# Two heads in one step: row-paired products of GLA and mLSTM inside a float32 block stack

## The chip, the cores and the metric

The kernel runs on one core of one Trainium2 chip. The metric is device time in microseconds (us), the median of several runs of the whole program, which is one launch. TensorE is called PE below, VectorE DVE, ScalarE ACT, GpSimd POOL and SyncE SP, as in the profile. All inputs and the output are float32.

## The reference, cut to what matters

Two blocks follow each other on one sequence of 1024 tokens of width 1024. The first is a recurrent mixer with its projections. The second holds a mixer with three branches (GLA, mLSTM, S5) and a feed-forward part. The change touches the two branches GLA and mLSTM, each with 4 heads whose keys and queries are 64 wide and whose values are 128 wide. In the reference they read

```python
# GLA, per chunk and head
o_inter = jnp.einsum('bhld,bhdv->bhlv', qi * jnp.exp(cum), state)
scores = jnp.einsum('bhid,bhjd,bhijd->bhij', qi, ki, decay)
o = o_inter + jnp.einsum('bhij,bhjv->bhiv', scores, vi)
# mLSTM, per chunk and head
scores = jnp.einsum('bhtd,bhsd->bhts', qi, ki) * jnp.exp(d_intra - m_t[..., None])
num = (w_inter[..., None] * jnp.einsum('bhtd,bhdv->bhtv', qi, mem)
       + jnp.einsum('bhts,bhsv->bhtv', scores, vi))
den = w_inter * jnp.einsum('bhtd,bhd->bht', qi, norm) + jnp.sum(scores, axis=-1)
h = num / jnp.maximum(jnp.abs(den), jnp.exp(-m_t))[..., None]
```

Products over the 64 key channels (scores, and query times state) contract 64 rows; products of the scores with the values contract the 128 tokens of a chunk.

## The kernel before, in words

The kernel works on 8 chunks of 128 tokens. A head pair (`hp` 0 or 1) shares one tile of 128 partitions: partitions 0 to 63 hold the key channels of head `h` = 0 of the pair, partitions 64 to 127 those of `h` = 1. A slice `r` picks one half, so a product over key channels uses one half of the array's rows.

The large projections are products of split float32 operands: each takes three products of 128 rows (`mm3`, L2457), and they form the main stream, whose PSUM tiles are named `mm` (4 buffers). GLA and mLSTM are generators that run beside that stream. The order of PE is written by hand: it executes in the order in which the Python code emits. After every 2500 ns of estimated main products (`tick` and `slot`, L2373 and L2382; usually 12 products of 512 columns) the generator at the head of the list `side` advances by one `yield`, at a rate of 1.08 per slot, so that about every 12th slot advances it twice without main work between. Generators in the list `fast` advance in every slot. The order of the other engines' instructions, and of the DMA queue on SP, comes from the framework's scheduler. Products outside the main stream go to PSUM tiles named `sm` (4 buffers, L2419). One float32 product shows as two records on PE, one for each pass.

GLA (`gla`, L1144) builds the score matrix of a head in 8 levels. `scores(l, h, wk, wq)` (L1181) makes, for one level and one head, two groups of four chunk products, each group in its own `sm` buffer, and copies each group into the tile `P` of that head: with a masked copy on DVE (L1203) for level 7 and levels 2 to 6, with ACT copies for levels 0 and 1 (whose products have 64 and 32 columns). There is a `yield` after each head. `weights` prepares the operand tile `w` of the next level. After the levels, for each head and each half of the chunks (`n4`), a product of `P` with the values `gv` (128 rows) and, for all but the first chunk, a product of the state (`S`, allocated as tile `kd`) with `qe` (allocated as tile `g`; 64 rows) accumulate alternately into one `sm` buffer. `head_norm` (L518) squares and scales that result into a tile `C`, and later transposes it.

mLSTM (`mlstm`, L1312) has eight steps per head pair, four per head, in a software pipeline: step `n` emits the scores of step `n` (`score`, L1454: two 64-row products into one buffer, then one DVE product into `mP`), the transposes of step `n`-2 (`finish`, L1484, from `mhn` into `my`), and the outputs of step `n`-1 (`numden`, L1465: 128-row products of `mP` with `mv`, and 64-row products of the state `mS` with `qw`, allocated as `mraw`, alternately), then yields. After the outputs, ACT takes an absolute value into `mdn`, DVE a maximum, a reciprocal and a product into `mhn`, which `finish` transposes. `rows_of` (L1391) loads the decay rows `mD` and the gate `mo` of a head.

Of the kernel before, what the change touches and what calls it, by code (L numbers as in the profile page):

```python
# [16 lines left out]
P = 128  # L17
# [103 lines left out]
class PhaseA:  # L121
# [395 lines left out]

    def head_norm(self, o, n, scale, dst, sp):  # L518

        ss = sp.tile([P, 4], F32, tag="hss", name=self.name("hss"), bufs=2)  # L520
# [12 lines left out]
        self.act(dst, ps[:, : n * P], AF.Copy)  # L533
# [10 lines left out]
class PhaseB:  # L544
# [599 lines left out]
    def gla(self):  # L1144
# [4 lines left out]
        def t_(name, shape, bufs=1):  # L1149
            return pool.tile([P] + list(shape), F32, tag=name, name=self.name(name), bufs=bufs)  # L1150
# [27 lines left out]
            self.mul(pr(w)[:, :, B : 2 * B], pr(d)[:, :, B : 2 * B], pr(q)[:, :, B : 2 * B])  # L1178
            return w

        def scores(l, h, wk, wq):  # L1181
            r = slice(h * 64, h * 64 + 64)
            B = LEVELS[l] if l < 7 else 0
            for n4 in range(2):
                ps = self.sm_ps()
                pt = pts[h][:, n4 * 4 : n4 * 4 + 4]
                p4 = ps.rearrange("p (n c) -> p n c", n=4)
                for j in range(4):
                    c0 = (n4 * 4 + j) * P
                    if B == 64:  # L1190
                        self.mm(p4[0:64, j, 64:P], wk[r, c0 : c0 + 64], wq[r, c0 + 64 : c0 + P])
                    elif B == 32:
                        for o in (0, 64):
                            self.mm(p4[o : o + 32, j, o + 32 : o + 64], wk[r, c0 + o : c0 + o + 32], wq[r, c0 + o + 32 : c0 + o + 64])
                    else:
                        self.mm(p4[:, j], wk[r, c0 : c0 + P], wq[r, c0 : c0 + P])
                if B == 64:
                    self.act(pt[0:64, :, 64:P], p4[0:64, :, 64:P], AF.Copy)
                elif B == 32:
                    for o in (0, 64):  # L1200
                        self.act(pt[o : o + 32, :, o + 32 : o + 64], p4[o : o + 32, :, o + 32 : o + 64], AF.Copy)
                else:
                    nc.vector.copy_predicated(pt, lm[:, l - 2].unsqueeze(1).broadcast_to([P, 4, P]), p4)  # L1203

        for hp in range(2):
            while ("gk", hp) not in self.zdone or "rows" not in self.zdone:
# [46 lines left out]
            yield  # L1253
            for l in range(7):
                nw = weights(l + 1, cum, q, k) if l < 6 else None
                for h in range(2):
                    scores(l, h, w, w)
                    yield
                    if l == 0:

                        if h == 0:
                            S = t_("kd", [T])
                        ps = self.sm_ps()
                        part = range(4 * h, min(4 * h + 4, NCH - 1))
# [13 lines left out]
                    yield  # L1278
                w = nw
            yield  # L1280
            for h in range(2):
                head = 2 * hp + h
                while ("gr", head) not in self.zdone:
                    yield
                r = slice(h * 64, h * 64 + 64)
                y = t_("w", [T], 2)
                gr, t = t_("d" if h else "kt", [T]), t_("e2", [T])
                nc.sync.dma_start(gr, self.z["gr"][head])
                norms = []
                for n4 in range(2):  # L1290
                    o = self.sm_ps()
                    for j in range(4):
                        n = n4 * 4 + j
                        oj = o[:, j * P : j * P + P]
                        self.mm(oj, pts[h][:, n], v[:, n, h * P : h * P + P], True, n == 0)
                        if n:
                            self.mm(oj, qe[r, n * P : n * P + P], S[r, n * P : n * P + P], False, True)
                    norms.append(self.head_norm(o, 4, 1.0 / P, y[:, n4 * H : n4 * H + H], pool))
                    next(norms[-1])
                    yield  # L1300
                self.act(t, gr, AF.Tanh, scale=0.5)
                self.stt(t, t, 1.0, gr, ALU.add, ALU.mult)
                for f in norms:
                    yield
                    for _ in f:
                        pass
                self.stt(y, y, self.col("gla_norm_w_2", head), t, ALU.mult, ALU.mult)
                nc.sync.dma_start(self.yd["gla"][head], y)
        pool.release()


    def mlstm(self):  # L1312
# [78 lines left out]
        def rows_of(head):  # L1391
# [9 lines left out]
            return d, mo, t_("my", [T], 2)  # L1401

        for hp in range(2):
            mk = yield from conv("mk", hp)
# [24 lines left out]
                    )  # L1429
            while ("mo", 2 * hp + 1) not in self.zdone:  # L1430
                yield
            nxt = rows_of(2 * hp)
            yield
            qw = t_("mraw", [T + 4], 2)[:, :T]
            for h in range(2):
                nc.sync.dma_start(qw[h * 64 : h * 64 + 64], bd[1, 2 * hp + h : 2 * hp + h + 1].broadcast_to([64, T]))
            self.stt(qw, mq, 0.5, qw, ALU.mult, ALU.mult)
            yield
            S = t_("mS", [NCH, 130])
            for n0 in range(0, NCH - 1, 3):  # L1440
                part = range(n0, min(n0 + 3, NCH - 1))
# [9 lines left out]
                yield  # L1451


            def score(h, n2, D):  # L1454
                r = slice(h * 64, h * 64 + 64)
                sc = self.sm_ps()
                pt = t_("mP", [2, P], bufs=2)
                for j in range(2):
                    n = n2 * 2 + j
                    c = slice(n * P, n * P + P)  # L1460
                    self.mm(sc[:, j * P : j * P + P], mk[r, c], mq[r, c])
                self.stt(pt.rearrange("p n c -> p (n c)"), sc[:, :256], 2.0 ** -5, D[:, n2 * 256 : n2 * 256 + 256], ALU.mult, ALU.mult)
                return pt

            def numden(h, n2, pt):  # L1465
                head = 2 * hp + h
                r = slice(h * 64, h * 64 + 64)
                o = self.sm_ps().rearrange("p (n c) -> p n c", n=2)
                for j in range(2):
                    n = n2 * 2 + j  # L1470
                    c = slice(n * P, n * P + P)
                    self.mm(o[:, j, 0:130], pt[:, j], v[h][:, n], True, n == 0)
                    if n:
                        self.mm(o[:, j, 0:130], qw[r, c], S[r, n], False, True)

                dn = t_("mdn", [2], bufs=2)
                self.act(dn, o[:, :, P], AF.Abs)
                self.tt(dn, dn, cols[:, 2, n2 * 2 : n2 * 2 + 2, head], ALU.max)
                nc.vector.reciprocal(out=dn, in_=dn)
                hn = t_("mhn", [2, P], bufs=2)  # L1480
                self.mul(hn, o[:, :, 0:P], dn.unsqueeze(2).broadcast_to([P, 2, P]))
                return hn

            def finish(h, n2, hn, mo, y):  # L1484
                ps = self.sm_ps()
                for j in range(2):
                    self.tr(ps[:, j * P : j * P + P], hn[:, j])
                c = slice(n2 * 256, n2 * 256 + 256)
                self.stt(y[:, c], mo[:, c], 1.0, ps[:, :256], ALU.add, ALU.mult)
                if n2 == 3:  # L1490
                    nc.sync.dma_start(self.yd["ml"][2 * hp + h], y)

            steps = [(h, n2) for h in range(2) for n2 in range(4)]
            have = {}
            for n in range(len(steps) + 2):
                if n < len(steps):
                    h, n2 = steps[n]
                    if n2 == 0:
                        have[h] = nxt
                        if h == 0:  # L1500
                            nxt = rows_of(2 * hp + 1)
                    have["pt", n] = score(h, n2, have[h][0])
                if n >= 2:
                    h, n2 = steps[n - 2]
                    finish(h, n2, have.pop(("hn", n - 2)), *have[h][1:])
                if 1 <= n <= len(steps):
                    have["hn", n - 1] = numden(*steps[n - 1], have.pop(("pt", n - 1)))
                yield
        pool.release()


# [1066 lines left out]
```

## Time and profile before

| what | value |
|---|---|
| median of 3 runs | 2270.28 us (2265.58 to 2273.81) |
| the profiled execution: its time | 2265.43 us |
| the profiled execution: its span, first to last instruction | 2263.6 us |
| mean granted PE clock over the span | 0.986 of full speed |
| PE busy | 2192.0 us, 97% of the span |
| DVE busy | 1514.4 us, 67% |
| ACT busy | 903.3 us, 40% |
| POOL busy | 394.7 us, 17% |

A row of a timeline gives the start from the span's start and the length in us, the engine, the line, the operation, the tile written and the tiles read, the shapes, and the number of records merged into the row; in brackets stands the idle time of the engine just before, and what ended it. The length of a PE row goes to the end of its last record, and records overlap, so the distance from one start to the next tells what a record costs. All PE products go through two helper lines, L2455 (matmul) and L2464 (transpose), so tile names tell them apart: `sm<-w` are GLA's scores of levels 0 to 6, `sm<-gq,gk` those of level 7, `sm<-gv,P` and `sm<-kd,g` GLA's outputs, `sm<-mq,mk` mLSTM's scores, `sm<-mv,mP` and `sm<-mS,mraw` its outputs, `sm<-ident,mhn` its transposes.

### The profile page before, as it was taken

The numbers are of one execution on the slowest core, as the hardware profiler recorded it, in microseconds if no ns is written. First come the engines' busy times: TensorE is split into PE (matmuls) and PEld (weight loads), VectorE is DVE, ScalarE is ACT, GpSimd is POOL, SyncE is SP. The second block draws the span as 40 slices with busy tenths as digits, with TensorE's granted clock in tenths as the row PEclk, the third lists the DMA queues.
The fourth block names the chain that finished last, engine by engine and source line by source line (L and its number), as shares of the span: only waits on it lengthen the run. The fifth ranks groups of instructions, "written<-read, shape, count | busy, mean of one in ns | idle before, by whom it ended". The sixth has DMA issues, their size and how long they took to land.

```text
span 2263.6 us, 29466 instructions
## 1 busy us (share of the span) xinstructions
PE 2192.0 (97%) x10998; PEld 1807.4 (80%) x10998; DVE 1514.4 (67%) x2160; ACT 903.3 (40%) x1522; POOL 394.7 (17%) x388
## 2 busy tenths in 40 slices
PE   8999999999999999999999999999799999999896
PEld 7888788887888988878887778887578888887676
DVE  6675686777486535558555346858977676779697
ACT  5553453344255544234253222446423232334343
POOL 1000000001112200000000000011745343425245
PEclk9999999999999999999999999999899999999998
DMA  4111116321743343255454255654233222267754
GB/s 172 34 44 40 40 51 205 103 61 29 224 144 115 98 145 136 98 170 166 152 172 143 79 183 181 202 180 153 88 123 110 84 84 84 98 228 253 246 177 160
DMA packets 149815, 297.59 MB, mean 131 GB/s; under 512 B 21520, under 2 KB 43936, under 8 KB 149416
## 3 DMA queue, kind: packets, MB, share of 16 engines
q1 hardware_dynamic: 135128, 271.33, 37.2%
q0 software_dynamic: 8128, 20.07, 2.5%
q10 hardware_dynamic: 6416, 4.31, 0.7%
q8 instruction: 87, 1.43, 0.3%
q14 instruction: 56, 0.46, 0.1%
HBM read 232.55 MB, written 61.90 MB: 130 GB/s over the span
## 4 chain that ended last, share of the span: by engine, by line
PE 76%; DVE 10%; DMA 5%; issue 5%; ACT 2%; POOL 2%; SPq 0%; POOLq 0%; ACTq 0%; DVEq 0%
PE mm L2455 56%; PE sm L2455 19%; DVE lo L2423 2%; DVE al L2423 1%; PE sm L2464 1%; DVE sc L2423 1%; DMA c<-ffa 1%; DVE res L2435 1%; DVE acc L2423 1%; POOL res L1843 1%; ACT hi L2449 0%; DVE B L2435 0%; DVE rl L2435 0%; DMA raw<-in_wfo 0%; ACT C L2449 0%
## 5 line engine op out<-in xcount | busy, mean ns | idle before, releaser
L2455 PE MATMUL mm<-rh,hi 128*128 128x512 f32 x1552 | 625.6, 403 | 1.1 <-DVE res L2423 0.7
L2455 PE MATMUL mm<-rl,hi 128*128 128x512 f32 x1552 | 606.2, 391 | 1.8 <-DVE rl L2423 1.8
L2455 PE MATMUL mm<-rh,lo 128*128 128x512 f32 x1552 | 606.7, 391 | 0.0
L2455 PEld LDWEIGHTS mm<-rh,hi 128*128 128x128 f32 x1552 | 292.5, 188 | 72.8 <-issue 9.5
L2455 PEld LDWEIGHTS mm<-rh,lo 128*128 128x128 f32 x1552 | 292.2, 188 | 62.8
L2455 PEld LDWEIGHTS mm<-rl,hi 128*128 128x128 f32 x1552 | 292.7, 189 | 61.7 <-issue 3.1
L2449 ACT ACTIVATE hi<-raw 128x1024 fp32r<-128x1024 f32 (+2 forms) x189 | 182.7, 970 | 369.3 <-PE mm L2455 265.7
L2423 DVE TENSOR_TENSOR lo<-raw,hi 128x1024 fp32r<-128x1024 f32 (+2 forms) x189 | 218.4, 1159 | 112.6 <-ACT hi L2449 110.3
L2455 PE MATMUL mm<-yr,hi 128*128 128x512 f32 x384 | 118.8, 390 | 0.2 <-DVE yr L2435 0.2
L2455 PE MATMUL mm<-tv,hi 128*128 128x512 f32 x312 | 102.5, 408 | 14.0 <-DVE tv L2423 7.1
L2455 PE MATMUL mm<-hi,rh 128*128 128x256 f32 (+1 forms) x384 | 110.7, 288 | 0.0
L2455 PE MATMUL mm<-hi,rl 128*128 128x256 f32 (+1 forms) x384 | 109.2, 284 | 0.0
L2455 PE MATMUL mm<-lo,rh 128*128 128x256 f32 (+1 forms) x384 | 109.2, 284 | 0.0
L1840 POOL TENSOR_TENSOR sl<-ru 128x512 f32<-128x512 f32 x22 | 37.1, 1689 | 315.7 <-DMA ru<-in_wfi 315.7
L2538 POOL TENSOR_TENSOR hss<-hss,mhalf 128x4 f32<-128x4 f32 x16 | 16.8, 1047 | 398.2 <-DVE hss L2441 292.1
L2455 PEld LDWEIGHTS mm<-tv,hi 128*128 128x128 f32 x312 | 61.1, 197 | 31.1 <-DVE tv L2423 9.4
L2455 PEld LDWEIGHTS mm<-yr,hi 128*128 128x128 f32 x384 | 72.1, 188 | 16.1 <-DVE yr L2435 1.1
L2449 ACT ACTIVATE hi<-sl 128x512 fp32r<-128x512 f32 x66 | 39.3, 626 | 108.9 <-PE sm L2455 66.6
L2435 DVE SCALAR_TENSOR_TENSOR adaa<-adar,cact,adaa 128x512 f32<-128x512 f32 x84 | 62.8, 747 | 29.8 <-DMA adar<-in_adaw 28.9
L2455 PEld LDWEIGHTS mm<-hi,rh 128*128 128x128 f32 x384 | 73.4, 191 | 1.7 <-issue 1.2
L2455 PE MATMUL mm<-yr,lo 128*128 128x512 f32 x192 | 74.7, 389 | 0.0
L2455 PEld LDWEIGHTS mm<-hi,rl 128*128 128x128 f32 x384 | 73.5, 191 | 0.7 <-issue 0.2
(526 smaller groups left out, 4356.7 us busy)
## 6 DMA issues: line engine op xcount, KB each, us to landing
raw<-in_w SPq DMA_DIRECT2D x60, 512.0 KB
adar<-in_adaw SPq DMA_DIRECT2D x96, 256.0 KB
c<-ffa SPq DMA_DIRECT2D x88, 256.0 KB
raw<-in_wfo SPq DMA_DIRECT2D x40, 512.0 KB
raw<-in_wfi SPq DMA_DIRECT2D x30, 512.0 KB
raw<-in_wo SPq DMA_DIRECT2D x24, 512.0 KB
ru<-in_wfi SPq DMA_DIRECT2D x22, 512.0 KB
raw<-in_wpj SPq DMA_DIRECT2D x32, 256.0 KB
```

Source lines behind the costliest of these rows:

```text
L1840: self.nc.gpsimd.tensor_tensor(out=out, in0=a, in1=b, op=ALU.add)
L1843: self.nc.gpsimd.tensor_tensor(out=out, in0=a, in1=b, op=ALU.subtract)
L2423: self.nc.vector.tensor_tensor(out=out, in0=a, in1=b, op=op)
L2435: self.nc.vector.scalar_tensor_tensor(out=out, in0=a, scalar=s, in1=b, op0=op0, op1=op1)
L2449: self.nc.scalar.activation(out=out, in_=a, func=f, scale=scale, **kw)
L2455: self.nc.tensor.matmul(out, lhsT=l, rhs=r, start=start, stop=stop)
L2464: self.nc.tensor.transpose(out, a, self.ident[:n, :n])
L2538: self.nc.gpsimd.tensor_tensor(out=out, in0=tmp, in1=self.mhalf[:, : out.shape[1]], op=ALU.pow)
```

## The change

GLA and mLSTM handle both heads of a pair in one step. In `scores`, a step is now one half of the chunks (`n4`) of both heads in place of both halves of one head: two `sm` buffers are taken first, and consecutive products go to head 0 and head 1 in turn, each to its own buffer. In the outputs of both branches the 128-row products of both heads come first, the 64-row products follow, alternating between the heads. mLSTM's pipeline has four steps per head pair in place of eight, with a second `yield` between `finish` and `numden`. The rows of the second head of a pair are loaded before the state is built, the gated result of mLSTM is written into `mo` in place of `my`, and `hss`, `mP`, `mdn` and `mhn` have four buffers in place of two. The number of `yield`s of each generator stays as it was (two per level and head pair, eight for GLA's outputs of a pair, ten for mLSTM's steps of a pair).

The diff, cut to its core:

```diff
-        def scores(l, h, wk, wq):
-            r = slice(h * 64, h * 64 + 64)
+        rows = [slice(h * 64, h * 64 + 64) for h in range(2)]
+        def scores(l, n4, wk, wq):
             B = LEVELS[l] if l < 7 else 0
-            for n4 in range(2):
-                ps = self.sm_ps()
...
+            p4s = [self.sm_ps().rearrange("p (n c) -> p n c", n=4) for _ in range(2)]
+            for j in range(4):
+                c0 = (n4 * 4 + j) * P
...
+                else:
+                    for r, p4 in zip(rows, p4s):
+                        self.mm(p4[:, j], wk[r, c0 : c0 + P], wq[r, c0 : c0 + P])
+            for h, p4 in enumerate(p4s):
                 pt = pts[h][:, n4 * 4 : n4 * 4 + 4]
...
+        def outputs(n4, v, qe, S):
+            os = [self.sm_ps() for _ in range(2)]
+            for h, o in enumerate(os):
+                for j in range(4):
+                    self.mm(o[:, j * P : j * P + P], pts[h][:, n4 * 4 + j], v[:, n4 * 4 + j, h * P : h * P + P], j == 0, False)
+            for j in range(4):
+                n = n4 * 4 + j
+                for r, o in zip(rows, os) if n else ():
+                    self.mm(o[:, j * P : j * P + P], qe[r, n * P : n * P + P], S[r, n * P : n * P + P], False, j == 3)
+            return os
...
-            for h in range(2):
-                scores(7, h, k, q)
+            for n4 in range(2):
+                scores(7, n4, k, q)
                 yield
...
+            norms = []
+            for n4 in range(2):
+                for h, o in enumerate(outputs(n4, v, qe, S)):
+                    norms.append((h, self.head_norm(o, 4, 1.0 / P, ys[h][:, n4 * H : n4 * H + H], pool)))
+                    next(norms[-1][1])
+                yield
+                yield
...
-            nxt = rows_of(2 * hp)
+            have = [rows_of(2 * hp)]
...
+            have.append(rows_of(2 * hp + 1))
...
+            def score(n2):
+                scs = [self.sm_ps() for _ in range(2)]
                 for j in range(2):
...
+                    for r, sc in zip(rows, scs):
+                        self.mm(sc[:, j * P : j * P + P], mk[r, c], mq[r, c])
...
+            def numden(n2, pts):
+                os = [self.sm_ps().rearrange("p (n c) -> p n c", n=2) for _ in range(2)]
+                for h, o in enumerate(os):
+                    for j in range(2):
+                        self.mm(o[:, j, 0:130], pts[h][:, j], v[h][:, n2 * 2 + j], j == 0, False)
                 for j in range(2):
...
+                    for r, o in zip(rows, os) if n else ():
+                        self.mm(o[:, j, 0:130], qw[r, c], S[r, n], False, j == 1)
...
+            for n in range(4 + 2):
+                if n < 4:
+                    sc[n] = score(n)
                 if n >= 2:
+                    finish(n - 2, hn.pop(n - 2))
                 yield
+                if 1 <= n <= 4:
+                    hn[n - 1] = numden(n - 1, sc.pop(n - 1))
+                    yield
```

## Rows read from the trace of the kernel before

**Rows 1.** The page, busy time of each engine over the span.
```profile
PE 2192.0 (97%) x10998; PEld 1807.4 (80%) x10998; DVE 1514.4 (67%) x2160; ACT 903.3 (40%) x1522; POOL 394.7 (17%) x388
```
**Rows 2.** What PE waited for from 860 to 1340 us: total, times, longest.
```profile
PE sm L2464 <- DVE mhn L2423: 2.2, 2, 1.2
PE mm L2455 <- DVE yr L2435: 0.2, 1, 0.2
```
**Rows 3.** Stretches: length, each engine's busy us, PE clock, DMA share, GB/s.
```profile
870.00:1140.00 270.00, 270.00 (x1571) 215.94 (x1570) 164.40 (x235) 95.63 (x196) 10.55 (x12) 1.00 0.44 145
...
1019.00:1055.00 36.00, 36.00 (x274) 28.79 (x273) 31.65 (x46) 18.86 (x34) 0.00 (x0) 1.00 0.58 182
```
**Rows 4.** PE groups by shape: count, then busy us, mean ns, idle before.
```profile
L2455 PE MATMUL sm<-w 64*128 64x128 f32 x320 | 40.4, 278 | 0.0
...
L2455 PE MATMUL sm<-gq,gk 64*128 64x128 f32 x64 | 8.2, 278 | 0.0
```
**Rows 5.** Timeline of PE: two main products, and two bursts of scores.
```profile
926.76 0.39 PE L2455 MATMUL mm<-rl,hi 128*128 128x512 f32 x1
926.99 0.39 PE L2455 MATMUL mm<-rh,lo 128*128 128x512 f32 x1
927.30 2.05 PE L2455 MATMUL sm<-w 64*128 64x128 f32 x16
...
944.12 3.50 PE L2455 MATMUL sm<-w 64*128 64x128 f32 x32
```
**Rows 6.** Timeline of PE, two steps of mLSTM without main work between.
```profile
1298.49 0.38 PE L2455 MATMUL sm<-mS,mraw 64*128 64x130 f32 x1
1298.50 0.37 PE L2455 MATMUL sm<-mq,mk 64*128 64x128 f32 x1
1298.71 0.27 PE L2455 MATMUL sm<-mS,mraw 64*128 64x130 f32 x1
1298.71 0.49 PE L2455 MATMUL sm<-mq,mk 64*128 64x128 f32 x3
1300.38 0.66 PE L2464 MATMUL sm<-ident,mhn 128*128 128x128 f32 x2 [1.17 <-DVE mhn L2423]
```
**Rows 7.** Timeline of PE, GLA's outputs of one head, both halves.
```profile
975.36 0.60 PE L2455 MATMUL sm<-gv,P 128*128 128x128 f32 x4
...
977.97 0.50 PE L2455 MATMUL mm<-rh,hi 128*128 128x512 f32 x1
...
980.83 0.38 PE L2455 MATMUL sm<-gv,P 128*128 128x128 f32 x2
...
984.05 0.50 PE L2455 MATMUL mm<-rh,hi 128*128 128x512 f32 x1
```
**Rows 8.** Timeline of PE, one step of mLSTM, to the next main product.
```profile
1285.54 0.71 PE L2455 MATMUL sm<-mq,mk 64*128 64x128 f32 x4
1286.18 0.44 PE L2464 MATMUL sm<-ident,mhn 128*128 128x128 f32 x2
1286.46 0.39 PE L2455 MATMUL sm<-mv,mP 128*128 128x130 f32 x2
...
1288.03 0.50 PE L2455 MATMUL mm<-rh,hi 128*128 128x512 f32 x1
```
**Rows 9.** Timeline of DVE, from an mLSTM output to its scaled result.
```profile
1288.34 0.16 DVE L2423 TENSOR_TENSOR mdn<-mdn,mcols 128x2 f32<-128x2 f32 x1 [1.26 <-ACT mdn L2449]
...
1288.81 0.42 DVE L2423 TENSOR_TENSOR mhn<-sm,mdn 128x256 f32<-128x256 f32 x1
```
**Rows 10.** Stretches around the two waits of mLSTM; columns as in rows 3.
```profile
1211.00:1219.00 8.00, 6.93 (x26) 4.74 (x25) 4.76 (x12) 1.92 (x3) 0.00 (x0) 0.79 0.48 133
...
1296.00:1308.00 12.00, 10.83 (x44) 8.04 (x43) 2.94 (x10) 0.34 (x2) 0.00 (x0) 0.72 0.25 87
```
**Rows 11.** Timelines of DVE and PE at GLA's start: masked copies, transposes.
```profile
893.94 2.62 DVE L1203 COPY_PREDICATED P<-lm,sm 128x512 f32<-128x512 uint32 x4
...
896.46 1.03 PE L2464 MATMUL sm<-ident,kd 128*128 128x128 f32 x8
```

More of the change, by code (lines that the diff above doesn't have):

```diff
@@ L1255, in gla @@
                 nw = weights(l + 1, cum, q, k) if l < 6 else None
-                for h in range(2):
-                    scores(l, h, w, w)
+                for n4 in range(2):
+                    scores(l, n4, w, w)
                     yield
                     if l == 0:
-                        if h == 0:
+                        if n4 == 0:
                             S = t_("kd", [T])
                         ps = self.sm_ps()
-                        part = range(4 * h, min(4 * h + 4, NCH - 1))
+                        part = range(4 * n4, min(4 * n4 + 4, NCH - 1))
                         for n in part:
@@ L1280, in gla @@
             yield
+            while ("gr", 2 * hp + 1) not in self.zdone:
+                yield
+            ys = [t_("w", [T], 2) for _ in range(2)]
+            grs = [t_(n, [T]) for n in ("kt", "d")]
             for h in range(2):
[L1282 to L1300, printed above, removed]
+                nc.sync.dma_start(grs[h], self.z["gr"][2 * hp + h])
+            norms = []
+            for n4 in range(2):
+                for h, o in enumerate(outputs(n4, v, qe, S)):
[3 more added lines that the diff above has]
+                yield
+            for h in range(2):
+                y, gr, t = ys[h], grs[h], t_("e2", [T])
                 self.act(t, gr, AF.Tanh, scale=0.5)
                 self.stt(t, t, 1.0, gr, ALU.add, ALU.mult)
-                for f in norms:
+                for f in (f for g, f in norms if g == h):
                     yield
@@ L1306, in gla @@
                         pass
[L1307 to L1308 removed]
+                self.stt(y, y, self.col("gla_norm_w_2", 2 * hp + h), t, ALU.mult, ALU.mult)
+                nc.sync.dma_start(self.yd["gla"][2 * hp + h], y)
         pool.release()
@@ L1451, in mlstm @@
                 yield
[L1454 to L1457, printed above, removed]
+            rows = [slice(h * 64, h * 64 + 64) for h in range(2)]
+            def score(n2):
+                scs = [self.sm_ps() for _ in range(2)]
                 for j in range(2):
@@ L1471, in numden @@
                     c = slice(n * P, n * P + P)
[L1472 to L1480, printed above, removed]
@@ L1493, in mlstm @@
[L1493 to L1502, printed above, removed]
+                    for r, o in zip(rows, os) if n else ():
+                        self.mm(o[:, j, 0:130], qw[r, c], S[r, n], False, j == 1)
@@ new lines, in numden @@
+                hns = []
+                for h, o in enumerate(os):
+                    dn = t_("mdn", [2], bufs=4)
+                    self.act(dn, o[:, :, P], AF.Abs)
+                    self.tt(dn, dn, cols[:, 2, n2 * 2 : n2 * 2 + 2, 2 * hp + h], ALU.max)
+                    nc.vector.reciprocal(out=dn, in_=dn)
+                    hn = t_("mhn", [2, P], bufs=4)
+                    self.mul(hn, o[:, :, 0:P], dn.unsqueeze(2).broadcast_to([P, 2, P]))
+                    hns.append(hn)
+                return hns
@@ new lines, in finish @@
+            def finish(n2, hns):
+                c = slice(n2 * 256, n2 * 256 + 256)
+                for h, hn in enumerate(hns):
+                    ps = self.sm_ps()
+                    for j in range(2):
+                        self.tr(ps[:, j * P : j * P + P], hn[:, j])
+                    mo = have[h][1]
+                    self.stt(mo[:, c], mo[:, c], 1.0, ps[:, :256], ALU.add, ALU.mult)
+                    if n2 == 3:
+                        nc.sync.dma_start(self.yd["ml"][2 * hp + h], mo)
@@ L1503, in mlstm @@
+            sc, hn = {}, {}
+            for n in range(4 + 2):
+                if n < 4:
+                    sc[n] = score(n)
                 if n >= 2:
[L1504 to L1507, printed above, removed]
+                    finish(n - 2, hn.pop(n - 2))
                 yield
+                if 1 <= n <= 4:
+                    hn[n - 1] = numden(n - 1, sc.pop(n - 1))
+                    yield
```

43 lines of the change are left out of this document (15 added, 28 removed).

## The prediction

> **What bounds the kernel now.** I read the page's busy times first: PE is busy for 97% of the span and no other engine for more than 67% [rows 1]. A high share alone doesn't make PE the bound, so next came what PE waited for in the stretch that the change touches: 2.4 us in 480, of which 2.2 on mLSTM's `mhn` [rows 2]. In GLA's stretch PE is busy for all of its 270 us at full clock [rows 3]. Whatever PE is spared there comes off the end, as long as no other engine turns late. The third look was at a 64-row product: half of the array's rows are idle in it, and the question is whether the other half can work at the same time.
>
> **How two halves share the array.** A burst of 16 score records lasts 2.05 us; less the 0.28 of the last record that is 1.77/16 = 0.111 us from record to record [rows 4, 5]. All records of such a burst use the same half of the rows. Two places show what happens where one half's products follow the other's, into another PSUM buffer. Two joined bursts, one per head, take 3.50 us for 32 records where 2.05 + 16 x 0.111 = 3.83 would be due: three records ran beside others [rows 5]. And the state product of one head and the score product of the other start 0.01 us apart, and once more at 1298.71 [rows 6]. So two halves do run side by side, weight loads included. In the old order they meet only where heads meet by chance.
>
> At 1298.50 the score product even starts ahead of the state product's second pass at 1298.71, which was emitted before it [rows 6], so one half needn't wait until a product of the other has done both passes. With 8 records per half, a burst of 16 then takes 8 places instead of 16. The Trainium skill, "TensorE: Matmul & The Clock Gate", Part 3, says that matmuls start and end strictly in program order; by that rule the halves would be offset by one pass and a burst would take 9 places. The row disagrees with the rule. By the rule the sum below would be smaller by one place in each of 52 bursts, some 6 us.
>
> **The change part by part.**
> *Scores.* Levels 2 to 6 have 320 records [rows 4], 20 bursts of 16. Each saves 8 x 0.111 = 0.89 us: 17.8, less the 0.33 already shared at 944, is 17.5. Level 7 has 64 records [rows 4], 4 bursts: 3.6. Level 0 has 4 bursts of 16 records with 64 columns, estimated at 64/128 of 0.111, so 8 x 0.056 x 4 = 1.8. Level 1 (32 columns) I take at 0.4; its bounds are 0 and level 0's 1.8. Together 23.3 us.
>
> *GLA's outputs.* One head takes 977.97 - 975.36 = 2.61 for its first half and 984.05 - 980.83 = 3.22 for its second [rows 7], so 5.83; four heads take 23.3. The second half has 16 records, 1.78 by the pure spacing; what is left, 1.44, is spread over 8 changes between 128 and 64 rows, 0.18 each. The new order changes twice per burst. Per pair and half: 16 records of 128 rows at 0.111 = 1.78, two changes 0.36, then the 64-row products in 6 places (no state product for chunk 0) or 8: 0.67 or 0.89. That is 2.81 + 3.03 = 5.84 per pair, 11.7 in all. Saved: 11.6. The Trainium skill, "TensorEngine Tiling (Array Packing)", Key Properties, has it that a change of tiling mode drains the engine; the 0.18 per change agrees.
>
> *mLSTM.* A full old step takes 1288.03 - 1285.54 = 2.49 [rows 8]: scores 0.64, two transposes 0.28, outputs 1.57. A pair has ten stretches between yields: scores alone (0.64), scores and a short output (1.70), six steps of 2.49 less 0.62 in the one whose chunk 0 has no state product, 1.79 and 0.14. Sum 18.6. The new ten: two of scores at 0.64 (eight records in four places), a short output at 1.5, three full ones at 8 x 0.111 + 0.36 + 4 x 0.111 = 1.7, two with scores and four transposes at 1.14, two with transposes at 0.5. Sum 11.2. Two pairs save 14.8.
>
> *What costs nothing.* `rows_of` of the second head moves ahead of the state products. Writing into `mo` makes the next pair's gate load wait for the store of this one, and weight loads stand behind it in SP's queue; they run four tiles ahead, 4 x 48 products x 0.23 [rows 5] = 44 us of main work. Gone, that cover would show as PE waiting for weights, of which there is nothing now [rows 2]. Four `C` tiles are held where two were, out of six; a main result needs one every 24 x 0.23 = 5.5 us, and four `mm` buffers hold back some 16 us before PE would wait.
>
> *What is late next.* Between a step's output and its transposes PE has one main run and one score stretch, 12 x 0.23 + 0.64 = 3.4 us. `mhn` is ready 1288.81 + 0.42 - 1288.03 = 1.2 us after the output [rows 8, 9]; a second head adds at most DVE's 0.89 (1288.34 to 1289.23), so 2.1. That fits, unless DVE is busy with something long or a slot advances twice without main work. The second happened at 1298: PE idled 1.17 us [rows 6] and its clock fell; the same at 1211, with 1.07 idle. The granted clock of those stretches was 0.72 and 0.79 [rows 10], so part of each ran at the lower level, 1.2 GHz. Idle time is 2.2 in all; with the clock's share, 0.28 x 12 + 0.21 x 8 = 5.0, it is 7.2, but idle and slow time overlap. I take 6, 3 per wait. The double slot falls at the same yield in the new order, between an output and its transposes, now with two heads to wait for: 3.7. The other wait I leave at 2.7.
> GLA's start gets tighter: the masked copies end at 893.94 + 2.62 = 896.56, 0.1 us after PE began the transposes of `kd` [rows 11]. Two level-7 bursts shorter by 0.89 bring PE there 1.8 us sooner, when its buffers are not free. Bounds: 0, if DVE's order shifts with it, and 1.8 per pair plus 2.5 of clock; I take 2 per pair, 4 in all. So waits cost 10.4 where they cost 6: 4.4 lost.
>
> *Sum.* 23.3 + 11.6 + 14.8 - 4.4 = 45.3 us. Against the profiled execution that is 2265.4 - 45 = 2220. The median of the runs lies 4.9 above that execution; on its scale the time is 2270.3 - 45.3 = 2225. GLA's outputs also interrupt the main stream in four places instead of eight, about 0.2 us each, so I say 2224.
>
> **The rivals.**
> *The halves share only for a few records.* The rows show three shared places in a row, not a burst. If sharing doesn't last, scores gain nothing and only the fewer changes are left: in GLA 7.4 per pair in place of 11.7 (1.78 + 0.36 + 1.33 or 1.78 per half), 8.5 saved; in mLSTM 14.6 in place of 18.6, 8.1 saved. That gives 2270 - 17 = 2253. Against it: the shared records were spaced like the others. 8%. The Trainium skill, "TensorE: Matmul & The Clock Gate", LDWEIGHTS, gives a load of 128 columns as columns / 1.2 GHz, 107 ns; were the loads of both halves served one after the other, this would be the result, and two products 0.01 us apart [rows 6] speak against it.
> *Late results of mLSTM.* If DVE's longer chain makes all eight pairs of transposes wait at 3 us each, 24 in place of the 6.4 in the sum, the time is 2224 + 18 = 2242. For it: DVE is busy for 31.65 of 36 us in one stretch of GLA [rows 3], so queues of 1 to 2 us occur. Against it: most steps leave 1.3 us. 10%.
> *Slower: the clock falls at the bursts.* If PE's clock fell after bursts with half as many places as it fell after the two waits, each fall would cost about 2.5 us (the 5.0 above, over two). There are 52 bursts (32 of scores, 4 of GLA's outputs, 16 in mLSTM). From 46/2.5 = 18 falls on the kernel is slower; all 52 give 2224 + 130 = 2354. Against it: the clock was granted in full over 270 us of GLA [rows 3], bursts included. 2%.
> *The change doesn't do what it says*, because a buffer is held back or another engine sets the pace of the side work: 2268. 2%.
>
> **How the numbers follow.** The forecast has 78%, the rivals 8, 10, 2 and 2. The forecast's own spread: with all waits gone 2224 - 10 = 2214, and the runs shown scatter by about 4 either way; one step further, if the halves pair better than counted, the lower end is 2206. The upper end takes in the late results with scatter, 2246, and leaves out the other rivals. A measurement of this kernel can tell a difference of about 0.3% (6.8 us) from no change. Faster by more than that: 0.95, within: 0.02, slower: 0.03.
>
> **What would show it.** Right: a score burst of 16 records lasts near 1.2 us instead of 2.05; outputs of a pair near 3 us per half; PE's idle time before the `mhn` and `kd` transposes a few us in total; main products still 0.23 apart. Wrong: score bursts still at 2 us (no sharing), a clock below 0.9 over GLA, PE waiting at every `mhn`, or waits for weights.

## The result: 2215.1 us, and the profile after

The changed kernel takes **2215.09 us** (median; runs from 2213.25 to 2217.10) against 2268.24 of the kernel before in the same comparison: ratio 0.9761, interval 0.9741 to 0.9781. It is faster by 53 us, 2.4%, where 46 were forecast (2224, between 2206 and 2246). A second comparison of the same kernel gave 2218.51, ratio 0.9765 [0.9744, 0.9785]. The profiled execution took 2213.25 us, its span 2211.4.

The page's busy times, to be held against [rows 1]:

```profile
PE 2138.3 (97%) x10998; PEld 1766.7 (80%) x10998; DVE 1511.8 (68%) x2160; ACT 900.2 (41%) x1522; POOL 394.7 (18%) x388
```

PE does the same 10,998 products in 53.7 us less busy time and still fills 97% of a span that is 52.2 shorter. It is still the bound, and no other engine's busy time moved by more than 3.1 us. Where it got shorter is in the PE groups by shape (count, busy us, mean ns, idle before and its releasers), which answer to [rows 4]:

```profile
L2471 PE MATMUL sm<-w 64*128 64x128 f32 x320 | 23.0, 284 | 0.0
...
L2480 PE MATMUL sm<-ident,mhn 128*128 128x128 f32 x32 | 5.5, 281 | 2.7 <-DVE mhn L2439 1.9 <-DVE mdn L1498 0.8
...
L2471 PE MATMUL sm<-gq,gk 64*128 64x128 f32 x64 | 4.6, 285 | 0.0
...
L2471 PE MATMUL sm<-w 64*64 64x64 f32 x64 | 3.0, 225 | 0.3 <-DVE P L1207 0.3
...
L2471 PE MATMUL sm<-w 64*32 64x32 f32 x128 | 1.8, 195 | 0.0
```

One score record lasts as long as before (284 ns, before 278), but the 320 together fill 23.0 us instead of 40.4: they overlap. The timeline of PE shows how, a burst of 16 with its weight loads (PEld), two joined bursts, GLA's outputs of a pair and a step of mLSTM (start, duration, idle before in brackets):

```profile
919.30 1.16 PE L2471 MATMUL sm<-w 64*128 64x128 f32 x16
919.30 0.97 PEld L2471 LDWEIGHTS sm<-w 64*128 64x128 f32 x16 [0.35 <-issue]
920.39 0.50 PE L2471 MATMUL mm<-rh,hi 128*128 128x512 f32 x1
...
937.50 2.06 PE L2471 MATMUL sm<-w 64*128 64x128 f32 x32
...
963.73 1.95 PE L2471 MATMUL sm<-gv,P 128*128 128x128 f32 x16
965.61 0.94 PE L2471 MATMUL sm<-kd,g 64*128 64x128 f32 x12
966.48 0.50 PE L2471 MATMUL mm<-rh,hi 128*128 128x512 f32 x1
...
972.49 1.95 PE L2471 MATMUL sm<-gv,P 128*128 128x128 f32 x16
974.37 1.16 PE L2471 MATMUL sm<-kd,g 64*128 64x128 f32 x16
975.46 0.50 PE L2471 MATMUL mm<-rh,hi 128*128 128x512 f32 x1
...
1189.56 0.72 PE L2471 MATMUL sm<-mq,mk 64*128 64x128 f32 x8
1190.21 0.66 PE L2480 MATMUL sm<-ident,mhn 128*128 128x128 f32 x4
1190.62 0.48 PE L2471 MATMUL mm<-rh,hi 128*128 128x512 f32 x1
...
1193.44 1.06 PE L2471 MATMUL sm<-mv,mP 128*128 128x130 f32 x8
1194.43 0.72 PE L2471 MATMUL sm<-mS,mraw 64*128 64x130 f32 x8
1195.08 0.50 PE L2471 MATMUL mm<-rh,hi 128*128 128x512 f32 x1
```

A burst of 16 lasts 1.16 us where it was 2.05 [rows 5]; less the last record, 0.88 / 0.111 = 7.9 places instead of 16. Its 16 weight loads are over in 0.97 us. GLA's outputs of a pair take 2.75 and 2.97 us, 5.72 in all, where one head took 5.83 [rows 7]. A full mLSTM step of both heads takes 1.06 + 1.64 = 2.70 where one head's took 2.49 [rows 8].

What PE waited for from 860 to 1300 us (total, times, longest), against [rows 2]:

```profile
PE sm L2480 <- DVE mhn L2439: 1.9, 3, 1.3
PE sm L2480 <- DVE kd L2439: 1.2, 1, 1.2
PE mm L2471 <- ACT yr L2465: 0.8, 1, 0.8
PE sm L2480 <- DVE mdn L1498: 0.8, 1, 0.8
...
PE sm L2471 <- DVE P L1207: 0.3, 1, 0.3
```

And stretches, with the columns of [rows 3]: GLA, the two places where mLSTM waits, as in [rows 10]:

```profile
869.00:1109.00 240.00, 238.53 (x1592) 188.78 (x1591) 163.32 (x236) 95.31 (x197) 10.05 (x11) 1.00 0.50 162
...
1178.00:1186.00 8.00, 6.66 (x42) 5.16 (x40) 3.88 (x13) 1.76 (x4) 0.00 (x0) 1.00 0.46 150
1246.00:1258.00 12.00, 10.86 (x73) 9.01 (x73) 4.80 (x18) 1.69 (x6) 0.00 (x0) 1.00 0.12 44
```

PE still stands idle in both places, 8.00 - 6.66 = 1.34 and 12.00 - 10.86 = 1.14 us, but the granted clock stays at 1.00, all at the 2.4 GHz level, where the kernel before was granted 0.79 and 0.72 [rows 10].

To put the 52 us of span into stretches, I take the same product of the main stream in both traces. The table gives by how many us it starts earlier than in the profiled execution of before; the last three columns are differences along a row. The waits from 860 to 1340 that fall into mLSTM stand beside them.

```
                     GLA    mLSTM   end of  last     gained in:            mLSTM's
                     start  start   mLSTM   product  GLA  mLSTM  later     waits on mhn/mdn
before starts at    871.5  1145.7  1322.9  2254.2                          2.2
changed                0.8   34.6    55.3    52.2   33.7   20.8   -3.1     2.7
changed, again        -1.9   32.3    51.7    46.2   34.2   19.4   -5.5     4.1
before, again         -2.0   -2.0    -0.4    -4.9    0.0    1.6   -4.5     2.2
scores only            0.6   22.3    25.5    20.8   21.7    3.2   -4.7     2.1
mLSTM only            -1.6   -1.6    20.2    16.7    0.0   21.8   -3.5     1.6
head by head          -1.6   17.9    38.0    35.1   19.6   20.1   -2.9     3.2
one half              -1.9    7.0    23.7    19.0    8.9   16.7   -4.7     0.5
change per chunk       0.6   30.7    49.3    45.2   30.1   18.6   -4.1     2.6
late mhn              -1.3   32.8    37.6    31.1   34.1    4.8   -6.5    14.0
more distance         -0.1   30.9    55.3    48.1   31.1   24.4   -7.2     0.0
mLSTM distance         0.4   34.5    58.9    52.6   34.2   24.4   -6.3     0.0
before, fewer changes -0.9   -0.9     8.4     1.6    0.0    9.3   -6.8     2.5
before, no wait       -2.3   -2.3     5.1    -5.3    0.0    7.4  -10.4     0.0
```

The row "before, again" gives the scatter of such a difference: 2.0 us at the start, 1.6 in mLSTM and 4.5 after it, with the same kernel. So GLA and mLSTM are read by their own columns, and "later", which is below zero in every row, is mostly how well the reference execution went.

### The profile page after: what moved, and what is told of

The parts are those of the page before. It is cut to its first block, busy times and chain, and to the rows that moved or that the text cites. A ratio compares the mean times of both kernels' runs of the same rounds, so it can differ in the third digit from the quotient of the medians.

```text
span 2211.4 us, 29459 instructions
## 1 busy us (share of the span) xinstructions
PE 2138.3 (97%) x10998; PEld 1766.7 (80%) x10998; DVE 1511.8 (68%) x2160; ACT 900.2 (41%) x1522; POOL 394.7 (18%) x388
## 4 chain that ended last, share of the span: by engine, by line
PE 73%; DVE 11%; issue 6%; DMA 5%; ACT 3%; POOL 2%; SPq 0%; POOLq 0%; DVEq 0%; ACTq 0%
PE mm L2471 55%; PE sm L2471 17%; DVE lo L2439 2%; DVE al L2439 2%; PE sm L2480 1%; DVE sc L2439 1%; POOL res L1859 1%; ACT hi L2465 1%; DVE acc L2439 1%; DMA ru<-in_wfi 1%; DVE rl L2451 1%; DMA adar<-in_adaw 1%; DMA mD<-mlrows 1%; DVE B L2451 0%; POOL lo L1859 0%
```

## The experiments

**Scores only** and **mLSTM only**: one part of the change each. The first keeps the kernel before and takes GLA's score bursts from the change; the second takes mLSTM's step alone.

```diff
-            for h in range(2):
-                scores(7, h, k, q)
+            for n4 in range(2):
+                scores(7, n4, k, q)
...
-                for h in range(2):
-                    scores(l, h, w, w)
+                for n4 in range(2):
+                    scores(l, n4, w, w)
```

```diff
-            steps = [(h, n2) for h in range(2) for n2 in range(4)]
...
+            sc, hn = {}, {}
+            for n in range(4 + 2):
```

> The kernel before with the new order in GLA's scores alone; GLA's outputs and mLSTM as before. Theory A (the two halves of the array work side by side): each burst of 16 score records takes 8 places of 0.111 us, 1.09 us to the next main product instead of 1.98; 24 such bursts and the 8 of levels 0 and 1 save 23.9 us, PE waits some 2 us at GLA's start, so 2246 against 2268 before. Rival B (the gain comes from fewer changes between 128-row and 64-row products): there is no such change inside a score burst, so bursts stay at 1.98 and the time at 2268.

> The kernel before with the new mLSTM alone; GLA as before. Theory A: mLSTM's stretch gets shorter by the same 20.8 us as in the changed kernel, so 2247 to 2248. Rival B: only the fewer changes count, some 8 us, 2260.

Measured: scores 2244.38 us, 0.9899 [0.9885, 0.9914], against 2267.9; mLSTM 2251.15, 0.9928 [0.991, 0.9945]. They save 23.5 and 16.8; the whole change saves 53.2, which leaves 12.9 for GLA's outputs (11.6 forecast). In the traces it is 33.7 - 21.7 = 12.0. The first came out within 2 us of its theory, and the scores' 23.3 stands. The second lies 3 us above its own, with runs from 2247.95 to 2254.70; in the trace mLSTM's stretch gains 21.8, as the theory has it (20.8).

**Head by head**: the records of head 1 are emitted after all of head 0's in a burst, as the two joined bursts of before stand; nothing else differs.

```diff
-            for j in range(4):
-                c0 = (n4 * 4 + j) * P
+            for r, p4 in zip(rows, p4s):
+                for j in range(4):
+                    c0 = (n4 * 4 + j) * P
...
-                for j in range(2):
-                    n = n2 * 2 + j
-                    c = slice(n * P, n * P + P)
-                    for r, sc in zip(rows, scs):
+                for r, sc in zip(rows, scs):
+                    for j in range(2):
```

> The changed kernel, but inside each burst all 64-row products of head 0 come first and those of head 1 after them, into the same two buffers. Theory A: the halves share only where the heads meet, three records as in the joined bursts of the kernel before, so a burst of 16 takes 13 places, 1.65 us instead of 1.09; with the outputs and mLSTM some 18 us are lost, 2233. Rival B: the number of changes is the same, so 2215.

Measured: 2229.8 us, 0.9833 [0.9818, 0.9847]. The timeline's burst of 16, and the group of mLSTM's scores:

```profile
922.83 1.71 PE L2469 MATMUL sm<-w 64*128 64x128 f32 x16
924.47 0.50 PE L2469 MATMUL mm<-rh,hi 128*128 128x512 f32 x1
```

```profile
L2469 PE MATMUL sm<-mq,mk 64*128 64x128 f32 x64 | 5.8, 296 | 0.0
```

(1.71 - 0.28) / 0.111 = 12.9 places: three records of one head's eight run beside the other's, as in the joined bursts of [rows 5]. So PE does run a product ahead of earlier ones of the other half, but only a few, and the order of emission is what makes the sharing complete. In mLSTM, where a head has four records per burst, the group fills 5.8 us (5.6 when they alternate), and the stretch gains 20.1 where it gained 20.8; that mLSTM lost so little would account for most of the 3 us by which this came out below its expectation.

**One half**: both heads' 64-row products take partitions 0 to 63, in two PSUM buffers and in alternation as in the changed kernel. Head 1's results are computed from head 0's keys and queries.

```diff
-        rows = [slice(h * 64, h * 64 + 64) for h in range(2)]
+        rows = [slice(0, 64) for h in range(2)]
```

> The changed kernel, but the 64-row products of head 1 (scores and state products of both branches) read head 0's partitions, so that part of the output is computed from head 0's data. Order, buffers and counts stay. Theory A: both heads' products need the same half of the array, nothing is shared, a burst of 16 takes 16 places, 1.98 us; 24 bursts at 0.89, level 0 at 1.8 in all, outputs and mLSTM some 11, so 34 lost: 2249. Rival C (it is the alternation between two PSUM buffers that speeds the products up, not the two halves): 2215.

Measured: 2244.6 us, 0.9898 [0.9882, 0.9915], with bursts as long as before:

```profile
924.32 2.05 PE L2471 MATMUL sm<-w 64*128 64x128 f32 x16
926.30 0.50 PE L2471 MATMUL mm<-rh,hi 128*128 128x512 f32 x1
```

Two buffers without two halves share nothing. The time came out 4 us below the 2249 expected. What is left of the gain, 23 us, goes with the order: by the table 8.9 in GLA, where the first rival had 8.5 for fewer changes of size, and 16.7 in mLSTM, where it had 8.1. There the waits all but went too (0.5 us, in the table), and with them the 7 us that they cost.

**Before again**, to see whether the clock's two falls recur:

> The kernel before once more, for a second profile. Open question: PE's clock fell after both of its waits for mhn. If such a wait brings the clock down by itself, both falls stand at the same two steps of mLSTM again, near 1215 and 1300 us, and the two cost some 6 us again. If the falls depend on something else, one or both are missing at the same waits.

One run, 2270.26 us. They do: waits of 2.2 on `mhn`, and the same two stretches (columns as in [rows 3]):

```profile
1214.00:1222.00 8.00, 6.99 (x29) 4.95 (x29) 3.96 (x10) 1.92 (x3) 0.00 (x0) 0.79 0.47 159
1299.00:1311.00 12.00, 10.83 (x52) 8.13 (x51) 3.86 (x13) 0.52 (x3) 0.00 (x0) 0.86 0.17 66
```

The second cost half as much (0.14 x 12 = 1.7 us lost instead of 0.28 x 12 = 3.4), and mLSTM's stretch was 1.6 us shorter. In "scores only", whose mLSTM is untouched, the waits were the same 2.1 us, the clock fell after the second alone, and the stretch was 3.2 shorter. What the clock costs thus comes on top of the idle time; it doesn't hide in it. The first wait of mLSTM in the second trace of before and in "scores only", and the stretch around the latter:

```profile
1215.32 0.44 PE L2464 MATMUL sm<-ident,mhn 128*128 128x128 f32 x2 [1.01 <-DVE mhn L2423]
```

```profile
1190.97 0.44 PE L2468 MATMUL sm<-ident,mhn 128*128 128x128 f32 x2 [0.98 <-DVE mhn L2427]
1187.00:1195.00 8.00, 7.02 (x34) 5.07 (x32) 6.36 (x13) 1.72 (x3) 0.00 (x0) 1.00 0.41 132
```

The same products wait equally long, 1.01 and 0.98 us; after the first the clock fell, after the second it didn't. So the old order itself doesn't always bring the fall.

**A change per chunk**: the outputs of the changed kernel, with 128-row and 64-row products in turn for each chunk, as before.

```diff
-            for h, o in enumerate(os):
-                for j in range(4):
-                    self.mm(o[:, j * P : j * P + P], pts[h][:, n4 * 4 + j], v[:, n4 * 4 + j, h * P : h * P + P], j == 0, False)
             for j in range(4):
                 n = n4 * 4 + j
+                for h, o in enumerate(os):
+                    self.mm(o[:, j * P : j * P + P], pts[h][:, n], v[:, n, h * P : h * P + P], j == 0, False)
```

> The changed kernel, but the outputs of GLA and mLSTM go chunk by chunk again: the 128-row products of both heads for one chunk, then their two 64-row products, side by side. Theory A with a price of 0.18 us per change between 128 and 64 rows: GLA's outputs have 6 or 8 changes per burst instead of 2, 1.8 us per pair, mLSTM's full outputs 4 instead of 2, 1.1 per pair; together 5.8 us, 2221. Rival B (the changes are what the kernel gained from): most of the gain of the outputs goes, 15 us or more, 2230. Rival: changes cost nothing, 2215.

Measured: 2221.45 us, 0.9798 [0.9777, 0.9818], 6.4 above the changed kernel. Its timeline in GLA:

```profile
974.53 0.71 PE L2469 MATMUL sm<-gv,P 128*128 128x128 f32 x4
975.17 0.49 PE L2469 MATMUL sm<-kd,g 64*128 64x128 f32 x4
```

Four 128-row records and the change take 975.17 - 974.53 = 0.64, less 4 x 0.111 = 0.20 per change; the forecast took 0.18. 20 changes more in GLA and 12 in mLSTM give 5.8 to 6.4; in the table GLA gains 3.6 less and mLSTM 2.2 less, 5.8.

**Late `mhn`**: the product that writes it is done four times on DVE, so that it comes late at every step.

```diff
-                    self.mul(hn, o[:, :, 0:P], dn.unsqueeze(2).broadcast_to([P, 2, P]))
+                    for _ in range(4):
+                        self.mul(hn, o[:, :, 0:P], dn.unsqueeze(2).broadcast_to([P, 2, P]))
```

> The changed kernel, but DVE writes each mhn four times with the same values, so that both heads' mhn are ready some 2 us later at each of the eight steps. Theory A: about 1.3 us of that is covered, each transposing step waits 0.7 to 1.2 us more and a wait costs its idle time: 6 to 10 us, 2221 to 2225. Rival (a wait costs 3 us because PE's clock falls after it, as I priced it): 24 us, 2236 or more, with granted clocks below 0.8 around the steps.

Measured: 2235.01 us, 0.9852 [0.9834, 0.9869], 19.9 above the changed kernel, between what the two theories gave and nearer to the rival. The waits, and the stretch of mLSTM with two parts of it:

```profile
PE sm L2481 <- DVE mhn L2440: 14.0, 9, 3.5
```

```profile
1182.00:1190.00 8.00, 4.48 (x16) 3.56 (x15) 6.26 (x18) 0.07 (x1) 0.00 (x0) 0.79 0.30 98
1260.00:1272.00 12.00, 8.72 (x56) 6.97 (x55) 4.96 (x19) 0.48 (x4) 0.00 (x0) 0.86 0.10 25
1110.00:1290.00 180.00, 165.79 (x880) 131.50 (x879) 98.34 (x203) 61.95 (x109) 0.79 (x8) 0.98 0.41 133
```

Nine waits, 14.0 us, and the clock fell only twice, the first time right after the longest of 3.52 us. The stretch loses 20.8 - 4.8 = 16.0 us: 14.0 - 2.7 = 11.3 more idle and 0.21 x 8 + 0.14 x 12 = 3.4 of clock make 14.7; 1.3 stay unexplained. A wait costs its own length, and now and then a fall of about 1.7. The 6 to 10 us of theory A were too small because the waits came out longer than it had them.

**More distance** and **mLSTM distance**: the second moves mLSTM's yields, so that two advances instead of one lie between an output and its transposes; the first has that too, and moves the last of GLA's three spare yields to before the transposes of `kd`.

```diff
                 if n < 4:
                     sc[n] = score(n)
+                if n < 5:
+                    yield
                 if n >= 2:
                     finish(n - 2, hn.pop(n - 2))
-                yield
                 if 1 <= n <= 4:
                     hn[n - 1] = numden(n - 1, sc.pop(n - 1))
                     yield
+                if n == 4:
+                    yield
```

More distance alone:

```diff
             self.mul(qe, qe, q)
+            yield
...
-                if l % 2:
+                if l in (1, 3):
                     yield
```

> The changed kernel with two moves and the same number of yields: in mLSTM the transposes of a step come one stretch later, just ahead of the next step's outputs, and in GLA one yield is moved from after level 5 to ahead of the transposes of kd. Theory A: the waits for mhn, 2.7 us, and for kd and the masked copies, 1.5 us, go: 2211. Rival: what made DVE late there makes PE wait somewhere else, 2215.

> The changed kernel with mLSTM's move of e8 alone: the transposes of a step come one stretch later, ahead of the next step's outputs; GLA as in the changed kernel. Theory A: mLSTM's stretch is 3.7 us shorter, as it was in e8, and nothing else moves: 2211 to 2212, faster than both kernels. Rival: what is saved there is lost at a later point of the program, as e8 lost 2 us and more after the stretch: 2215.

Measured: 2219.39 us, 0.9785 [0.9767, 0.9803], and 2213.05, 0.9744 [0.9726, 0.9761]. The first is slower than both its theory and its rival had it, the second lies between the two. In both, mLSTM's waits are gone and its stretch gains 24.4 instead of 20.8. With more distance, GLA gives 2.6 back. Its timeline there, and the stretch around it:

```profile
1031.07 0.50 PE L2475 MATMUL sm<-w 64*32 64x32 f32 x34
1034.52 0.65 PE L2475 MATMUL sm<-w 64*32 64x32 f32 x30 [2.95 <-DVE kd L2455]
1035.10 0.79 PE L2475 MATMUL mm<-rh,hi 128*128 128x512 f32 x1
```

```profile
1030.00:1042.00 12.00, 9.05 (x96) 7.02 (x97) 9.19 (x14) 6.91 (x15) 0.00 (x0) 0.86 0.65 205
```

A double advance now falls between two bursts of scores, PE waits 2.95 us for `kd`, and the next main product lasts 0.79 instead of 0.50: over these 12 us (columns as in [rows 3]) the granted clock was 0.86, so for part of them 1.2 GHz. With mLSTM's distance alone the wait comes later, at the first products after mLSTM:

```profile
1275.24 0.50 PE L2474 MATMUL mm<-yr,hi 128*128 128x512 f32 x1 [1.36 <-ACT yr L2468]
```

With a fall of the clock there (0.86 over the 12 us from 1272), 3.4 us of the lead go (58.9 at mLSTM's end, 55.5 at the 5217th main product); the changed kernel loses 1.5 in the same place. The version is the fastest measured: 5.5 us below the changed kernel beside it, 2.0 below that kernel's first median, with runs that overlap those of both (2211.78 to 2215.31). Its lead over the changed kernel is thus near the scatter and not settled.

**Before, with fewer changes**, and **before, without the waits**: two parts of the explanation tried on the old order. The first emits each head's two 128-row products before its 64-row ones; the second finishes an mLSTM step one advance later, with a third `mhn` buffer.

```diff
                 for j in range(2):
+                    self.mm(o[:, j, 0:130], pt[:, j], v[h][:, n2 * 2 + j], j == 0, False)
+                for j in range(2):
...
-                    self.mm(o[:, j, 0:130], pt[:, j], v[h][:, n], True, n == 0)
                     if n:
-                        self.mm(o[:, j, 0:130], qw[r, c], S[r, n], False, True)
+                        self.mm(o[:, j, 0:130], qw[r, c], S[r, n], False, j == 1)
```

```diff
-                hn = t_("mhn", [2, P], bufs=2)
+                hn = t_("mhn", [2, P], bufs=3)
...
-                if n >= 2:
-                    h, n2 = steps[n - 2]
+                if n >= 3:
+                    h, n2 = steps[n - 3]
```

> The kernel before, but in each mLSTM output step the two 128-row products come first and the two 64-row products after them; still one head per step. Two changes fewer in each of 12 full outputs at 0.18 us: 4.3 us. PE still waits about as long for mhn. If such a wait brings the clock down by itself: both falls again, 2264. If the fall also needs the thinly filled outputs around the wait: none, 2260.

> The kernel before, but mLSTM's transposes come one step later (a third buffer for mhn), so that PE has no wait for mhn. My price of the two waits with their clock falls is 6 us: 2262. If the waits cost their idle time alone, 2.2 us: 2266.

Measured: fewer changes 2262.97 us, 0.9966 [0.9952, 0.998], between the two forecasts. The old waits are still there (2.5 us), but in the one trace of it no fall follows. The timeline, and the two stretches:

```profile
1214.34 0.44 PE L2465 MATMUL sm<-ident,mhn 128*128 128x128 f32 x2 [1.10 <-DVE mhn L2424]
...
1296.28 0.41 PE L2465 MATMUL sm<-ident,mhn 128*128 128x128 f32 x2 [1.39 <-DVE mhn L2424]
```

```profile
1210.00:1218.00 8.00, 6.90 (x35) 5.12 (x33) 6.73 (x13) 1.74 (x3) 0.00 (x0) 1.00 0.34 117
1290.00:1302.00 12.00, 10.61 (x61) 8.13 (x60) 5.17 (x16) 1.58 (x5) 0.00 (x0) 1.00 0.24 87
```

The stretch gains 9.3 us. Two changes fewer in each of the 12 steps that have state products in both chunks are 24 x 0.18 = 4.3; the falls of before are 5.0 [rows 10]; less 0.3 of longer waits that makes 9.0.

No wait: 2270.47 us, 1.0006 [0.9995, 1.0017]. That is a miss: both theories expected a gain. Mean clock 1.00 and no idle time at 1211, and 7.4 us gained by the end of mLSTM; but then:

```profile
1329.38 0.49 PE L2455 MATMUL mm<-yr,hi 128*128 128x512 f32 x1 [1.59 <-ACT yr L2449]
1330.11 0.50 PE L2455 MATMUL mm<-yr,hi 128*128 128x512 f32 x1 [0.23 <-DVE yr L2435]
...
1333.76 1.52 PE L2455 MATMUL mm<-yr,hi 128*128 128x512 f32 x2 [2.75 <-ACT yr L2449]
```

```profile
1211.00:1219.00 8.00, 8.00 (x38) 5.94 (x37) 7.12 (x13) 2.46 (x6) 0.00 (x0) 1.00 0.26 100
1326.00:1340.00 14.00, 9.43 (x30) 6.38 (x30) 6.28 (x10) 6.14 (x10) 0.00 (x0) 0.76 0.76 233
```

PE stands 4.6 us for `yr` where it stood 0.2 [rows 2], the clock falls (0.76), and 7.1 of the 7.4 us are gone by the 5217th main product. The wait was moved, not removed: mLSTM now takes one advance more per pair, and the loads of the branch results that `yr` is made of stand behind it in the list `side`. The last wait of 2.75 us ends 0.7 us after such a load has landed.

**The changed kernel again**, beside the last three:

> The changed kernel once more, beside e9 on the same chip: 2215 within 2, no clock fall between 1110 and 1270 us, waits of mhn near 2.7 us in all.

Measured: 2218.51 us, 0.9765 [0.9744, 0.9785]. Its mLSTM waits 4.1 us, longest 2.67, without a fall of the clock (1.00 from 1178 to 1190 and from 1248 to 1260). The time and the waits lie outside what was expected of them, the clock doesn't. With its waits added back the stretch gains 19.4 + 4.1 = 23.5; the first profile gives 20.8 + 2.7 = 23.5, mLSTM only 21.8 + 1.6 = 23.4. That is the part that scatters least.

## Why the prediction was right, and which term was off

- **Halves share the array, weight loads included**: right. The burst takes 7.9 places (8 forecast, from three shared records in a row), and one half alone takes 16. The order of emission isn't kept across the halves: head by head, head 1's first product starts three records before head 0's eight are done, so ahead of head 0's last product, which is two records. By the rule cited from the Trainium skill, "TensorE: Matmul & The Clock Gate", Part 3, the burst would have taken 9 places, and head by head nothing could have run ahead; both came out otherwise. But the 9 count each pass of a product as a matmul of its own. By whole products the pairs in [rows 6] and in the burst can start and end in order, so what disagrees with the rule is head by head, and the joined bursts of [rows 5], more than the row that the prediction named. The 16 weight loads of the burst took 0.97 us. By the 107 ns of a load in the Trainium skill, "TensorE: Matmul & The Clock Gate", LDWEIGHTS, 16 loads one after the other would fill 1.7 us, an estimate.
- **Scores, 23.3**: right, by groups: 17.4 for levels 2 to 6 (17.5 forecast), 3.6 for level 7 (3.6), 1.6 for level 0 (1.8), 1.0 for level 1 (0.4, between the bounds given).
- **GLA's outputs, 11.6**: right, 11.9 by the timeline (5.72 per pair against 2 x 5.83). The price of a change, 0.18, measured 0.20 when 32 were put back.
- **mLSTM's products, 14.8**: a little too small. By difference, 23.5 without the waits less the 7.2 that waits and falls cost before (below), they saved 16.3. A step came out at 1.06 + 1.64 where 1.14 + 1.7 were taken; added up in the timeline, waits taken out, the ten stretches of a pair took 10.8 and 10.4 where 11.2 were forecast, which makes 16.0.
- **Waits, 10.4 after against 6 before, so 4.4 lost**: this term failed, in sign. Before, they cost 2.2 of idle time and 0.21 x 8 + 0.28 x 12 = 5.0 of clock, 7.2 together; removing them gained 7.4. The prediction took 6, since it let idle and slow time overlap; they don't. After, mLSTM waits 2.7 and GLA 1.5, 4.2 in all, with no fall. The price of 3 per wait had a fall in each. The double advance came where it was forecast, and cost 0.83 + 0.31 = 1.14 of idle time where 3.7 were taken. So waits gave 7.2 - 4.2 = 3.0 back instead of taking 4.4, a difference of 7.4. In idle time alone they did take 2.0; the gain is the 5.0 of clock, and that part is of this pair of traces: the old mLSTM lost 3.4 to the clock in its second trace and 1.7 in "scores only".
- **Sum**: in GLA 23.6 + 11.9 - 1.5 (its waits) = 34.0, and the table shows 33.7; mLSTM shows 20.8. The stretch ahead of GLA gives 0.8 and 3.1 are lost after mLSTM, half of it by the 5217th main product, where PE waits for `yr`, the rest in the last 200 us, far from the change: 52.2. The forecast's 45.3 plus the 7.4 of the waits is 52.7; that one term is the miss. That the other deviations cancel, some 2 too small in the products against the time lost after mLSTM, for which the prediction had no term, is chance.
- **What was to cost nothing** cost nothing: no wait for weights in the stretch, and none on a `C` tile.
- **The rivals.** Sharing for a few records only fell with the bursts. Late results at every step were produced in an experiment and cost 16 us in the stretch. That is near the 18 of that rival by luck: its price of 3 was some 1.1 of idle time and the rest clock, while here the waits were 1.6 on average and the clock fell twice, not eight times. The kernel doesn't do it: it waits at three steps, not eight. The clock didn't fall at bursts: 1.00 over GLA's 240 us. And the change does what it says.

What stays open is why waits of 1.01 to 1.17 us in the old order were followed by a lower clock in both profiles of the kernel before, while 0.98 in the same order ("scores only"), 1.10 and 1.39 in the old order with fewer changes, and 1.34 and 2.67 in the new one, were not. The length of the wait doesn't decide it. That PE works more densely around the wait in the new order is only argued, and that it is chance from one execution to the next is a rival that no run here rules out: there are only one or two traces of each version.

## What to carry to other kernels

Where products use 64 rows and there are two independent ones, emit them in turn on the two halves, into two PSUM buffers, and put products of one size together: here a burst halved, and each change of size avoided was worth 0.2 us. Price a removed wait by its idle time plus the clock it cost, and then look at what is late next: in the old order 7.4 us were won by moving two waits away and 7.1 lost again at the next stage. A wait that a trace shows with a fall of the clock shouldn't be carried to another order at that price, because the fall may not come along.

## What the runs showed of the hardware that was not expected

- PE's reach ahead is short: emitted head by head, a burst of 16 needed 13 places, and in bursts of 4 + 4 records the group of scores lost almost nothing (5.8 us against 5.6).
- The sharing hangs on the rows. Two PSUM buffers on the same rows gave 2.05 us per burst, as one buffer did.
- The granted clock doesn't follow single waits: nine waits of 14.0 us in all gave two falls, two of 2.2 us gave two, and the same two, 2.1 us, gave one in "scores only". A fall cost 1.7 us or 3.4, by the granted clock of its stretch, on top of the idle time.
